# Three edits to one inference step of a hybrid trunk: activation rows of 388 columns, the last squares added ahead of the statistics, a packed product for the pool's shift

## The chip, the core and the metric

The kernel is one program on one core of a Trainium2 chip. The metric is the device time of one execution in microseconds. The names of engines are those of the profile: PE is TensorE (PEld its weight loads), DVE is VectorE, ACT is ScalarE, POOL is GpSimd, SP is SyncE, whose queue issues nearly all transfers (SPq). L521 is line 521 of the kernel before.

## What is computed

384 tokens (128 context tokens and 256 latent ones, each group with a conditioning vector of its own) go through four layers. Layers 0 and 3 mix tokens with a gated MLP in chunks (gMLP), layer 1 with centred pooling, layer 2 with windowed attention; each is followed by a feed-forward part with a width-3 convolution. Each sub-layer begins with an RMS norm and an adaLN scale and shift:

```python
def rms_norm(x, g):
    xf = x.astype(jnp.float32)
    y = xf * lax.rsqrt(jnp.mean(xf * xf, axis=-1, keepdims=True) + EPS)
    return (y * g.astype(jnp.float32)).astype(x.dtype)
...
        h = rms_norm(x, g_mix[i]) * (1 + sc1) + sh1
        if kind == 0:
            y = chunk_gmlp(h, a_w_in[j], a_g_v[j], a_w_s[j], a_b_s[j], a_w_out[j])
        elif kind == 1:
            y = multi_pool(h, p_w[j], p_b[j], p_scale[j])
...
        x = x + gt1 * y
        h = rms_norm(x, g_ffn[i]) * (1 + sc2) + sh2
        x = x + gt2 * conv_ffn(h, w_ffn_in[i], ffn_conv_w[i], ffn_conv_b[i], w_ffn_out[i])
```

The pooling mixer takes, for each of four groups of 256 features, the mean of h over a window of 2, 4, 8 or 16 tokens less h itself, and multiplies by a 256 x 256 matrix of the group.

## The kernel before

**Layout.** Features lie on partitions: x is 8 tiles (k or d, 0 to 7) of 128 features by 384 tokens. Weights stream in as chunks of 128 x 1024 float32 into five buffers (wraw, one SP transfer each). Each is split into two float32r parts: ScalarE rounds it (whi, L338), VectorE takes the remainder (wlo, L345). Activations are split in the same way into a high and a low part. A product is three passes, hi*hi, lo*hi and hi*lo (mm3, L631 to L638).

**hh and hl.** They hold a norm's operand for all eight feature tiles, 128 x 8 x TE with TE = 386: 384 tokens of x * g * (1 + sc), then two columns with the shift of each token group. A product with 386 moving columns so gives the shift's product beside the tokens', and the norm's factor (one per token) is applied after it. prep (L570) fills a tile d as soon as x_d is final: hh by ScalarE (L586), hl by VectorE (L588), then the square of x_d by ScalarE. VectorE adds the squares to acc (L468), but those of the last tile are only returned as sq. In layer 0's gMLP the products read the first 384 columns of the same rows.

**Statistics.** stats (L515) sums the squares over partitions by products with ones into cs: for each of three token tiles one product with acc and one with sq (L521). VectorE and ScalarE make 1/rms of it (L524, L508 to L512), VectorE a diagonal R of it (L530), and TensorE spreads R over all partitions (L536). This happens between the products of two feature tiles of the next phase: before tile 5, in layer 1's feed-forward part before tile 7 (stat_k), in layer 3's gMLP before tile 2.

**The pool** (L900 to L975). Its constants mx (mix) and the column sums ms (mixsum, two rows of 4 x 384) are loaded as it starts, into space that the feed-forward part before it has held. For a group g, first(g) makes the product with the group's weights, tokens on partitions; its fourth block is the shift's product, two rows (L929). scaled(g) copies the token blocks with the factor 1/rms (ScalarE, L938) and the two rows of the shift (VectorE, L940) to u. second(g) makes, for the group's two feature tiles, the product of u with the constants: a float32 product over two rows for the shift (L949), then three over tokens (L950, L953). VectorE adds the result to x (L956), and prep's work on that tile follows. The order is first(0), stats, first(1), scaled(0), first(2), scaled(1), second(0), scaled(2), first(3), second(1), scaled(3), second(2), second(3).

**What sets the order.** The program's text does: each engine runs its instructions in the order in which they are written, and waits on semaphores; SP's queue too. The pool's stretch of TensorE's chain begins at 540.38 us of the profile and ends where the feed-forward part's products begin, at 570.00.

Of the kernel before, what the change touches and what calls it, by code (L numbers as in the profile page):

```python
# [9 lines left out]
F32 = mybir.dt.float32  # L10
# [9 lines left out]
KD = 8  # L20
T = 384
# [13 lines left out]
TE = T + 2  # L35
BUFS = 5
# adaLN sections (layer, which of the six) computed along with the weights of a phase: by VectorE ("ad", features on
# partitions, dot products along the free axis) or by TensorE ("ap", column-tiled products)
# [18 lines left out]
# chunks of a phase that none of VectorE's sections follow, at its start and at its end  # L57
EDGES = {(0, "gv"): (2, 1), (0, "go"): (5, 0), (3, "gv"): (5, 2), "fi": (0, 6), (3, "go"): (5, 2)}

# the same for those of TensorE, at the end  # L60
# [4 lines left out]
# ---------------------------------------------------------------- packing  # L65


def out_chunks(fam, j, nk):
    """Two feature tiles at a time, but the last two one after the other."""
# [5 lines left out]
def weave(ws, es, lead, rest):  # L75
    """Spread es evenly over ws, but for the first `lead` and the last `rest`."""
# [13 lines left out]
def chunk_plan():  # L90
    """Chunks of 128 x 1024 in the order in which the program loads them: (family, index)."""
# [126 lines left out]
def shape_consts():  # L218
    """Constants that depend on shapes alone: rope tables, window mask, a selection matrix."""
# [20 lines left out]
def pool_mix():  # L240
    """mix[t', g, t]: weight of token t' in the centred mean at t, less one where t' = t."""
# [17 lines left out]
def pool_sums():  # L259
    """Column sums of mix for each group of tokens (what a shift common to all its tokens is weighed with)."""  # L260
# [7 lines left out]
# ---------------------------------------------------------------- program  # L268


class Prog:
# [36 lines left out]
    # ---- stream of chunks  # L308
# [4 lines left out]
    def load(self, most=BUFS):  # L313
        """Start the loads for which there is room."""
# [14 lines left out]
    def w_split(self, upto, mid=None):  # L329
        """Round the coming chunks (ScalarE), run mid, take the remainders (VectorE)."""  # L330
# [38 lines left out]
    # ---- adaLN parameters  # L369
# [37 lines left out]
    def ada_spare(self, n):  # L407
        """At most n of VectorE's chunks, of those already loaded."""
        for _ in range(n):
            if self.queue["ad"] and self.queue["ad"][0] in self.raw:  # L410
                self.ada_dve()
# [16 lines left out]
    def ada_fill(self, n, fin=True):  # L428
        """At most n products of those already loaded; without fin, none that would have to close a section before."""
# [17 lines left out]
    # ---- norm  # L447
    def residual(self, d, ps, l, ty, after):
        """x_d += gate * ps, and what follows from x_d."""
# [9 lines left out]
    def square(self, d, acc):  # L459
        """Add the squares of x_d to acc; the last ones are only returned."""  # L460
# [9 lines left out]

# [1111 lines left out]
```

## Time and profile before

| what | value |
|---|---|
| time, median of 3 runs | 1800.54 us (1800.51 to 1800.55) |
| profiled execution: span from first to last instruction | 1798.9 us |
| TensorE busy | 1778.0 us (99%), 10458 products |
| VectorE busy | 1364.0 us (76%) |
| ScalarE busy | 862.5 us (48%) |
| GpSimd busy | 1.8 us |
| mean DMA rate | 173 GB/s |

The span is that of one profiled execution; the runs' times are of other executions and include what lies before the first and after the last instruction. Busy times of products overlap, so the distance from one start to the next tells what a product costs, not its listed duration. A float32 product counts as two instructions (two passes), a float32r product as one.

### The profile page before, as it was taken

The page shows a single profiled execution, that of the slowest core. Times are in us where ns is not written, and L with a number is a line of the kernel's source. Part 1 is how long each engine was busy: PE and PEld are TensorE (multiplying, and loading weights), DVE is VectorE, ACT ScalarE, POOL GpSimd, SP SyncE. Part 2 cuts the span into 40 slices and gives each one's busy share as a digit, 9 for nine tenths or more (in the row PEclk, how much of TensorE's full clock was granted, in tenths as well). Part 3 has the DMA queues.
Part 4 walks back from the last instruction along what each step waited for, and adds up shares of the span by engine and source line. Part 5 has one row for each costly group of instructions (what it writes and reads, how often), then busy time and mean ns, then how long its engine had stood idle before and what let it go on. Part 6 is the DMA issues. An engine that isn't in the chain of part 4 may idle for free.

```text
span 1798.9 us, 27205 instructions
## 1 busy us (share of the span) xinstructions
PE 1778.0 (99%) x10458; PEld 1685.6 (94%) x10458; DVE 1364.0 (76%) x2568; ACT 862.5 (48%) x1470; POOL 1.8 (0%) x30
## 2 busy tenths in 40 slices
PE   7999999999999999999999999999999999999999
PEld 5799899999998999999678999999988999999999
DVE  5877688887776888776777788878776787888732
ACT  3634335554445555432568454544354443545431
POOL 0000000000000000000000000000000000000000
PEclk9999999999999999999999999999999999999999
DMA  8875565554553444365643444436546245444341
GB/s 321 281 243 178 211 219 182 184 177 157 205 182 118 152 153 164 135 211 184 241 171 124 145 154 154 162 135 211 193 161 213 96 163 188 141 145 148 123 148 58
DMA packets 87639, 311.67 MB, mean 173 GB/s; under 512 B 10451, under 2 KB 10963, under 8 KB 87253
## 3 DMA queue, kind: packets, MB, share of 16 engines
q1 hardware_dynamic: 87364, 309.92, 49.7%
q8 instruction: 82, 1.34, 0.3%
q14 instruction: 49, 0.39, 0.1%
q10 hardware_dynamic: 144, 0.01, 0.0%
HBM read 308.06 MB, written 1.84 MB: 172 GB/s over the span
## 4 chain that ended last, share of the span: by engine, by line
PE 96%; DVE 2%; ACT 1%; DMA 1%; issue 0%; DVEq 0%; ACTq 0%
PE mm L638 76%; PE mm L763 6%; PE S L1036 2%; PE S L638 1%; PE psa L398 1%; PE mm L807 1%; PE adaT L638 1%; PE mm L929 1%; PE psa L763 1%; PE adaT L763 1%; PE Tps L1036 1%; PE cs L521 1%; PE O L1256 0%; PE psa L638 0%; PE psa L1438 0%; PE Tps L1244 0%
## 5 line engine op out<-in xcount | busy, mean ns | idle before, releaser
L345 DVE TENSOR_TENSOR wlo<-wraw,whi 128x1024 fp32r<-128x1024 f32 (+2 forms) x390 | 466.0, 1201 | 212.2 <-ACT whi L338 207.1
L338 ACT ACTIVATE whi<-wraw 128x1024 fp32r<-128x1024 f32 (+2 forms) x390 | 400.7, 1036 | 388.4 <-PE mm L638 307.1
L638 PE MATMUL mm<-hh,whi 128*128 128x386 f32 (+1 forms) x1664 | 427.2, 342 | 0.0
L638 PE MATMUL mm<-hh,wlo 128*128 128x386 f32 (+1 forms) x1664 | 423.5, 339 | 0.0
L638 PE MATMUL mm<-hl,whi 128*128 128x386 f32 (+1 forms) x1664 | 421.2, 338 | 0.0
L638 PEld LDWEIGHTS mm<-hh,whi 128*128 128x128 f32 x1664 | 300.0, 188 | 7.9 <-issue 4.9
L638 PEld LDWEIGHTS mm<-hh,wlo 128*128 128x128 f32 x1664 | 303.4, 188 | 0.0
L638 PEld LDWEIGHTS mm<-hl,whi 128*128 128x128 f32 x1664 | 303.2, 188 | 0.0
L380 DVE SCALAR_TENSOR_TENSOR junk<-wraw,condb 128x1024 bf16<-128x1024 f32 x240 | 293.3, 1222 | 7.1 <-ACT condb L1500 2.7
L638 PE MATMUL mm<-gh,whi 128*128 128x384 f32 x704 | 193.6, 336 | 0.0
L638 PE MATMUL mm<-gh,wlo 128*128 128x384 f32 x704 | 193.6, 336 | 0.0
L638 PE MATMUL mm<-gl,whi 128*128 128x384 f32 x704 | 193.5, 336 | 0.0
L638 PEld LDWEIGHTS mm<-gh,wlo 128*128 128x128 f32 x704 | 128.5, 188 | 0.0
L638 PEld LDWEIGHTS mm<-gh,whi 128*128 128x128 f32 x704 | 128.5, 188 | 0.0
L638 PEld LDWEIGHTS mm<-gl,whi 128*128 128x128 f32 x704 | 128.4, 188 | 0.0
L682 ACT ACTIVATE ct<-ct 128x385 f32<-128x385 f32 x88 | 46.4, 528 | 156.7 <-DVE ct L676 156.6
L676 DVE SCALAR_TENSOR_TENSOR ct<-ab,par,ct 128x385 f32<-128x385 f32 x176 | 108.9, 621 | 12.2 <-ACT ct L674 8.2
L685 DVE SCALAR_TENSOR_TENSOR gg<-u,be,ct 128x128 f32<-128x128 f32 (+1 forms) x176 | 65.6, 416 | 47.6 <-ACT ct L682 47.6
L586 ACT ACTIVATE hh<-x,A 128x128 fp32r<-128x128 f32 x96 | 43.2, 457 | 102.5 <-DVE x L453 91.6
L672 ACT ACTIVATE ab<-a,be 128x128 f32<-128x128 f32 (+1 forms) x176 | 70.0, 446 | 28.9 <-DVE be L659 28.9
L657 DVE TENSOR_TENSOR a<-mm,rbs 128x384 f32<-128x384 f32 x88 | 48.7, 553 | 37.7 <-PE mm L638 31.8
L674 ACT ACTIVATE ct<-ab,par 128x385 f32<-128x385 f32 x88 | 62.7, 712 | 3.4
(302 smaller groups left out, 1987.6 us busy)
## 6 DMA issues: line engine op xcount, KB each, us to landing
wraw<-wts SPq DMA_DIRECT2D x562, 512.0 KB, 3.3
wraw<-wts SPq DMA_DIRECT2D x12, 256.0 KB, 2.5
wraw<-wts SPq DMA_DIRECT2D x8, 384.0 KB, 3.5
x<-x SPq DMA_DIRECT2D x4, 384.0 KB, 4.5
mx<-mix SPq DMA_DIRECT2D x1, 1280.0 KB, 8.1
y<-x SPq DMA_DIRECT2D x3, 384.0 KB, 3.1
condb<-condb SPq DMA_DIRECT2D x1, 1024.0 KB, 8.1
ws<-a_w_s SPq DMA_DIRECT2D x2, 512.0 KB, 4.2
```

Of the source, the lines that this page charges most:

```text
L338: nc.scalar.activation(hi[:, :n], t[:, :n], AF.Copy)
L345: nc.vector.tensor_tensor(out=lo[:, :n], in0=t[:, :n], in1=hi[:, :n].bitcast(F32), op=ALU.subtract)
L380: nc.vector.scalar_tensor_tensor(out=self.junk.bitcast(BF16), in0=w, scalar=1.0, in1=self.condb[:, c, :], op0=ALU.mult, op1=ALU.mult, accu ...
L638: nc.tensor.matmul(o, w[:, c:c + nw], r, start=(first and p == 0), stop=(last and p == 2))
L657: nc.vector.tensor_tensor(out=a1, in0=pa[:, 0:T], in1=rbs, op=ALU.mult)
L672: nc.scalar.activation(ab[:, p0:p1], a1[:, t0:t1], AF.Identity, bias=be[:, c:c + 1])
L674: nc.scalar.activation(t, ab[:, 1:T + 2], AF.Identity, scale=cw[1], bias=cb)
L676: nc.vector.scalar_tensor_tensor(out=t, in0=ab[:, i:i + T + 1], scalar=cw[i], in1=t, op0=ALU.mult, op1=ALU.add)
L682: nc.scalar.activation(t, t, GELU)
L685: nc.vector.scalar_tensor_tensor(out=g[:, t0:t1], in0=u1[:, t0:t1], scalar=be[:, 2 + c:3 + c], in1=t[:, t0 + c:t1 + c], op0=ALU.add, op1=A ...
L763: nc.tensor.matmul(ps[n][i], hs, w[p == 1][:, c:c + 512], start=(k == 0 and p == 0), stop=(k == 7 and p == 2))
L1036: nc.tensor.matmul(ps[i], hs, w[p == 1][:, c:c + 512], start=(k == 0 and p == 0), stop=(k == 7 and p == 2))
```

## The change

- hh and hl get rows of TP = 388 columns; the last two are never read. Products still have 386 columns (or 384 in layer 0).
- In each feed-forward part and in layer 3's gMLP, VectorE adds sq to acc (add_square) before the phase's first weights are asked for, and stats takes acc alone. The pool's and attention's statistics still take both.
- In the pool, the shift's product becomes one float32r product over 128 rows. msr holds the column sums rounded in rows 0, 1 and 32, 33 and the remainder in rows 64, 65; ush holds the shift's rows rounded in 0, 1 and 64, 65 and their remainder in 32, 33; all other rows are zero (filled by GpSimd). One pass so gives hi*hi, lo*hi and hi*lo.
- The small tiles dmy and ms have one buffer instead of two. Comments are gone.

```diff
+TP = T + 4
...
+    def add_square(self, pr):
+        self.nc.vector.tensor_tensor(out=pr["acc"], in0=pr["acc"], in1=pr["sq"], op=ALU.add)
...
-        d = self.tmp.tile([128, 1], F32, tag="dmy", name="dmy")
+        d = self.tmp.tile([128, 1], F32, tag="dmy", name="dmy", bufs=1)
...
-        m = self.tmp.tile([128, 3], F32, tag="ms", name="ms")
+        m = self.tmp.tile([128, 3], F32, tag="ms", name="ms", bufs=1)
...
             b = [self.bank()[:, :TE] for _ in range(4)]
+            self.add_square(pr)
             for kk in range(4):
                 w = self.w_get("fr")
...
-                        R = self.diag(self.stats(pr["acc"], pr["sq"]))
+                        R = self.diag(self.stats(pr["acc"]))
...
                 rbs = None
+                self.add_square(pr)
...
-                            R = self.diag(self.stats(pr["acc"], pr["sq"]))
+                            R = self.diag(self.stats(pr["acc"]))
...
-                        self.mm3([(b[i], 512 * k2 + 128 * i) for i in range(4)], w, (self.hh[:, k, :], self.hl[:, k, :]),
+                        self.mm3([(b[i], 512 * k2 + 128 * i) for i in range(4)], w,
+                                 (self.hh[:, k, 0:TE], self.hl[:, k, 0:TE]),
...
             nc.sync.dma_start(ms, self.a["mixsum"])
+            msr = pp.tile([128, 4, T], F32R, tag="msr", name="msr")
+            ush = pp.tile([128, 4, 256], F32R, tag="ush", name="ush")
+            nc.gpsimd.memset(msr.bitcast(F32), 0.0)
+            nc.gpsimd.memset(ush.bitcast(F32), 0.0)
+            for q in (0, 32):
+                nc.vector.tensor_copy(msr[q:q + 2], ms)
+            nc.vector.tensor_tensor(out=msr[64:66], in0=ms, in1=msr[0:2].bitcast(F32), op=ALU.subtract)
             res, aft = prep()
...
-                u = pp.tile([128, 4, 256], F32, tag="u", name="u", bufs=3)
+                u = pp.tile([128, 3, 256], F32, tag="u", name="u", bufs=3)
...
-                nc.vector.tensor_copy(u[0:2, 3, :], ps[1][0:2, 256:512])
+                for q in (0, 64):
+                    nc.vector.tensor_copy(ush[q:q + 2, g, :], ps[1][0:2, 256:512])
+                nc.vector.tensor_tensor(out=ush[32:34, g, :], in0=ps[1][0:2, 256:512], in1=ush[0:2, g, :].bitcast(F32),
+                                        op=ALU.subtract)
...
-                    nc.tensor.matmul(ps, u[0:2, 3, c], ms[:, g, :], start=True, stop=False, skip_group_check=True)
+                    nc.tensor.matmul(ps, ush[:, g, c], msr[:, g, :], start=True, stop=False, skip_group_check=True)
...
-        self.hh = self.const.tile([128, KD, TE], F32R, name="hh")
-        self.hl = self.const.tile([128, KD, TE], F32R, name="hl")
+        self.hh = self.const.tile([128, KD, TP], F32R, name="hh")
+        self.hl = self.const.tile([128, KD, TP], F32R, name="hl")
```

Where VectorE's instructions stand as the pool begins, before (x of the feed-forward part's last tile is just split into hh and hl; A are the gains, cs the statistics' sums, u the scaled copy):

```order
L588 SCALAR_TENSOR_TENSOR hl<-x,A,hh 128x256 [waits Activation_49]
L544 SCALAR_TENSOR_TENSOR A<-prm,par 128x16
L345 TENSOR_TENSOR wlo<-wraw,whi 128x1024 [waits DMAHW2_49,Activation_49]
L524 TENSOR_SCALAR ms<-cs 128x3 [waits PE_49]
L509 RECIPROCAL rs_5138<-rs_5137 128x3 [waits Activation_49]
...
L512 SCALAR_TENSOR_TENSOR rs_5140<-rs_5139,rs_5138 128x3 [waits DVE_49]
L940 COPY u<-mm 2x256 [waits Activation_49]
```

The same place in the changed kernel:

```order
L593 SCALAR_TENSOR_TENSOR hl<-x,A,hh 128x256 [waits Activation_49]
L926 CAST msr<-ms 2x1536 [waits DMAHW0_49,Pool_49]
L926 CAST msr<-ms 2x1536
L927 TENSOR_TENSOR msr<-ms,msr 2x1536 [waits DVE_49]
L549 SCALAR_TENSOR_TENSOR A<-prm,par 128x16
L346 TENSOR_TENSOR wlo<-wraw,whi 128x1024 [waits DMAHW2_49,Activation_49]
L529 TENSOR_SCALAR ms<-cs 128x3 [waits PE_49]
...
L517 SCALAR_TENSOR_TENSOR rs_5145<-rs_5144,rs_5143 128x3 [waits DVE_49]
L958 CAST ush<-mm 2x256 [waits Activation_49,Pool_49]
L958 CAST ush<-mm 2x256
L959 TENSOR_TENSOR ush<-mm,ush 2x256 [waits DVE_49]
```

Three operations over 1536 columns, the first of which waits for a transfer and for GpSimd, now stand ahead of the gains, a remainder and the statistics; one copy per group became two casts and a subtraction.

TensorE's statistics in layer 0's feed-forward part, before:

```order
L638 MATMUL mm<-hl,whi 128x386 x4
L521 MATMUL cs<-ones,acc 128x1 [waits PE_49]
L521 MATMUL cs<-ones,sq 128x1 [waits Activation_49]
L521 MATMUL cs<-ones,acc 128x1
L521 MATMUL cs<-ones,sq 128x1
L521 MATMUL cs<-ones,acc 128x1
L521 MATMUL cs<-ones,sq 128x1
L638 MATMUL mm<-hh,whi 128x386 x4
```

And in the changed kernel:

```order
L643 MATMUL mm<-hl,whi 128x386 x4
L526 MATMUL cs<-ones,acc 128x1 [waits DVE_49,PE_49]
L526 MATMUL cs<-ones,acc 128x1 x2
L643 MATMUL mm<-hh,whi 128x386 x4
L643 MATMUL mm<-hh,wlo 128x386 x4
```

Six products (twelve passes) became three, and they wait for VectorE's addition where they waited for ScalarE's square.

## Rows read from the trace of the kernel before

**Rows 1.** The page, part 4: the chain that ended last, by engine.

```profile
PE 96%; DVE 2%; ACT 1%; DMA 1%; issue 0%; DVEq 0%; ACTq 0%
```

**Rows 2.** Groups by form, TensorE: line, names, shapes, count | busy us, mean ns.

```profile
L638 PE MATMUL mm<-hh,whi 128*128 128x386 f32 x1536 | 393.1, 341 | 0.0
```

**Rows 3.** The chain in order of time: start us, us, what; gMLP and attention products.

```profile
164.21 8.44 PE mm L638 x48
...
995.34 16.66 PE S L638 x96
```

**Rows 4.** Timeline, TensorE, layer 2's feed-forward: start us, us; first product of each tile.

```profile
1047.58 0.52 PE L638 MATMUL mm<-hh,whi 128*128 128x386 f32 x2
...
1048.63 0.53 PE L638 MATMUL mm<-hh,whi 128*128 128x386 f32 x2
...
1049.70 0.51 PE L638 MATMUL mm<-hh,whi 128*128 128x386 f32 x2
...
1050.76 0.52 PE L638 MATMUL mm<-hh,whi 128*128 128x386 f32 x2
...
1051.83 0.52 PE L638 MATMUL mm<-hh,whi 128*128 128x386 f32 x2
...
1052.90 0.51 PE L638 MATMUL mm<-hh,whi 128*128 128x386 f32 x2
...
1053.96 0.51 PE L638 MATMUL mm<-hh,whi 128*128 128x386 f32 x2
...
1055.01 0.51 PE L638 MATMUL mm<-hh,whi 128*128 128x386 f32 x2
...
1056.07 0.52 PE L638 MATMUL mm<-hh,whi 128*128 128x386 f32 x2
```

**Rows 5.** The chain in order of time: statistics in layer 0's feed-forward part.

```profile
264.50 1.24 PE cs L521 x12
```

**Rows 6.** Timeline, TensorE, layer 1's feed-forward part: [idle before <-releaser].

```profile
589.33 0.88 PE L536 MATMUL adaT<-R,ones 128*128 128x384 f32 x2 [1.05 <-DVE R L530]
```

**Rows 7.** Groups by form, VectorE.

```profile
L468 DVE TENSOR_TENSOR acc<-acc,sq 128x384 f32<-128x384 f32 x42 | 23.5, 559 | 3.6 <-ACT sq L466 3.6
...
L800 DVE TENSOR_SCALAR v<-v,rd 128x512 f32<-128x512 f32 x16 | 6.6, 480 | 0.1
...
L940 DVE COPY u<-mm 2x256 f32<-2x256 f32 x4 | 1.6, 410 | 2.4 <-ACT u L938 2.4
```

**Rows 8.** Timeline, VectorE, start of layer 0's feed-forward part.

```profile
260.02 1.22 DVE L345 TENSOR_TENSOR wlo<-wraw,whi 128x1024 fp32r<-128x1024 f32 x1 [0.88 <-ACT whi L338]
```

**Rows 9.** The chain in order of time: first product of second(0), first of the feed-forward part.

```profile
550.21 0.84 PE mm L949 x2
...
570.00 12.72 PE mm L638 x72
```

**Rows 10.** Timeline, VectorE, the pool: a remainder; sums into two neighbouring feature tiles.

```profile
543.93 1.23 DVE L345 TENSOR_TENSOR wlo<-wraw,whi 128x1024 fp32r<-128x1024 f32 x1 [1.62 <-ACT whi L338]
...
564.79 0.72 DVE L956 SCALAR_TENSOR_TENSOR x<-mm,pgs,x 128x128 f32<-128x128 f32 x2
...
566.98 0.74 DVE L956 SCALAR_TENSOR_TENSOR x<-mm,pgs,x 128x128 f32<-128x128 f32 x2
```

**Rows 11.** Timeline, SP's queue: the issue of the pool's constants.

```profile
540.46 0.33 SPq L909 DMA_DIRECT2D mx<-mix  x1
```

**Rows 12.** The page, part 6: transfers, KB each, median us from issue to landing.

```profile
mx<-mix SPq DMA_DIRECT2D x1, 1280.0 KB, 8.1
```

**Rows 13.** Timeline, ScalarE, the pool: the first scaled copies.

```profile
546.38 1.20 ACT L938 ACTIVATE u<-mm,rs 128x256 f32<-128x256 f32 x3 [0.92 <-DVE rs L512]
```

**Rows 14.** The chain in order of time: the start of the kernel.

```profile
10.79 1.45 PE cs L521 x6
...
18.21 2.69 PE mm L763 x6
...
22.25 4.38 PE mm L763 x18
```

More of the change, by code (lines that the diff above doesn't have):

```diff
@@ L788, in vnorm @@
             def vnorm():
-                m = self.tmp.tile([128, 3], F32, tag="ms", name="ms")
+                m = self.tmp.tile([128, 3], F32, tag="ms", name="ms", bufs=1)
                 nc.vector.tensor_reduce(out=m, in_=ss, op=ALU.add, axis=AX.X)
@@ L1269, in store_lo @@
                                         op=ALU.subtract)
-            nc.scalar.activation(self.tmp.tile([128, 1], F32, tag="dmy", name="dmy"), self.ones[:, 0:1], AF.Exp)
+            nc.scalar.activation(self.tmp.tile([128, 1], F32, tag="dmy", name="dmy", bufs=1), self.ones[:, 0:1], AF.Exp)
             put(2)
@@ L1500, in hook @@
                 nc.scalar.activation(self.condb, self.condb, AF.Silu)
-                nc.scalar.activation(self.tmp.tile([128, 1], F32, tag="dmy", name="dmy"), self.ones[:, 0:1], GELU)
+                nc.scalar.activation(self.tmp.tile([128, 1], F32, tag="dmy", name="dmy", bufs=1), self.ones[:, 0:1], GELU)
         pr = None
```

## The prediction

> **What bounds the kernel.** The chain of work that ended last comes first: 96% of it is TensorE's [rows 1], so time is won or lost only where TensorE's products get fewer or shorter, or where it waits. The table of groups then says which products these are: 3 x 1536 = 4608 have 386 moving columns out of hh or hl [rows 2]. To see what one costs, I read starts, not the listed durations, since products overlap. 48 products of 384 columns out of hh (rows of 386) took 8.44 us, 175.8 ns each; 96 out of qS, whose rows are 384 long, took 16.66 us, 173.5 ns each [rows 3]. In the feed-forward stream, a block of 48 products of 386 columns runs from 1047.58 to 1056.07 us, 8.49 us or 176.9 ns each, and nothing is idle in it [rows 4].
>
> **Pitch 388.** No instruction is added. Two columns more than 384 should cost 173.5 x 386/384 = 174.4 ns; the block shows 176.9, so up to 2.5 ns of each product can be put down to where its row starts: 4608 x 2.5 = 11.5 us, all on the path. That is one end. The other is 0: if the number of columns does it, it stays. The block itself tells more. Each of its listed starts opens a feature tile k (six products). Counted from the start of hh, even k begin at multiples of 16 bytes already (3088 bytes per two rows), odd ones 8 bytes past one. Even tiles (the first listed and every second) took 1.05 + 1.06 + 1.07 + 1.05 = 4.23 us for 24 products, 176.25 ns; odd ones 1.07 + 1.07 + 1.06 + 1.06 = 4.26, 177.5 ns. If odd tiles only become like the even ones, each product gains half of 1.25, 0.63 ns, 2.9 us in all. But an even tile always follows an odd one, and a slow product can push the next, so I take the middle between 2.9 and 11.5: **-7.2 us**. No row excludes a loss by itself, but even tiles are not the slower ones, so I put the lower end at 0. Layer 0's 384 products of 384 columns show 175.8 against 173.5, 2.3 ns, 0.9 us at most; half of it, **-0.4**. ScalarE and VectorE write the same shapes at other offsets: nothing, and they are not on the path.
>
> The row above leaves even tiles 1.9 ns dearer than 174.4. The Trainium skill (SBUF — State Buffer, "SBUF: two separate sides", the note on cachelines) says that SBUF is read in lines of 16 bytes and that each access that crosses to a new line pays. By that rule a row of 386 float32, 96.5 lines, touches 97 whether it starts on a line or 8 bytes into one; pitch 388 would then give nothing for the 4608 products, and the sum would be that of the second rival below. The small difference of even and odd tiles speaks for it, layer 0's 384 columns neither way.
>
> **Squares added ahead.** Where both partial sums went into the statistics, six products run as twelve passes, 1.24 us of the chain [rows 5]; with one sum it is half, 0.62 us. It is done at five places: the four feed-forward parts and layer 3's gMLP. In layer 1's feed-forward TensorE waits 1.05 us right behind for VectorE's diagonal [rows 6]; there it would only wait longer, so that one is worth nothing. 4 x 0.62 = **-2.5 us**. The added VectorE addition has the shape of one of 559 ns [rows 7]; it stands where VectorE idles 0.88 us before its next remainder [rows 8], so I cost it at nothing. Without that cover, the first remainders of the next weights would come 0.6 us later, and they are chunks ahead of use. In layer 1 VectorE is late already and 0.6 us would show. The ms and dmy tiles with one buffer are rewritten long after their last reader: nothing.
>
> **Pool's packed product.** On TensorE, each of eight float32 products of two passes takes 0.84 us [rows 9]; one single-pass product of 384 columns takes 0.17 [rows 3]. 8 x 0.67 = 5.3 us less, if nothing else is late. Two things are.
> First, VectorE: a feature tile there costs 566.98 - 564.79 = 2.2 us [rows 10] against TensorE's 2.12, which falls to 1.45, so VectorE becomes the bound of the second half. The last two products need the last group's casts, which stand behind four tiles and two sets of three small copies (0.41 us each [rows 7]): 1.45 + 4 x 2.2 + 6 x 0.41 + 2 x 1.45 = 15.6 us from the first of these products to the feed-forward part, where 570.00 - 550.21 = 19.8 stand now [rows 9]. So 4.2 less; I take 4.0 for hand-overs.
> Second, the preparation of msr: two casts and a subtraction of 1536 columns stand on VectorE ahead of the gains, and wait for ms. The mixsum transfer is issued behind mix, at 540.46 [rows 11], on the same queue; mix takes 8.1 us to land [rows 12], so ms is there at about 548.6. A SBUF operation of 512 columns takes 480 ns [rows 7], a cast of 1536 by proportion 1.44; the subtraction is one and a half remainders of 1.23 us [rows 10], 1.85. VectorE is free at 548.6 + 4.7 = 553.3. Queued behind are the gains (a sixteen-column operation, 0.2), a remainder, the statistics' refinement and, on ScalarE, the three scaled copies: from 543.93 [rows 10] to 546.38 + 1.20 = 547.58 [rows 13], 3.65 us. The first packed product can start at 557.1 instead of 550.2: TensorE idles 6.9 us. If the casts go at twice that rate, it is 5.5; if they go at the subtraction's, 7.8; if ms landed at its issue, there is no stall, and the pool gains its 4.0. GpSimd's two fills have no row of that size; they start with the transfers, and I take them as done within its 8 us. Together 6.9 - 4.0 = **+2.9 us**.
>
> **Sum.** -7.2 - 0.4 - 2.5 + 2.9 = -7.2 us. The span of the profiled execution is 1798.9 us; the median of the runs is 1800.54, and 1.6 us lie outside the span. Put on the median: **1793.3 us**, with an own range of 1790 to 1797.5 (the ends of the casts and half of the pitch's uncertainty). About 0.2%, 3.6 us, is what a measurement of this kernel can tell from no change.
>
> **Rivals.**
> *The whole excess goes.* All rows of 388 then read like rows of 384: -11.5 - 0.9 - 2.5 + 2.9 = -12.0, 1788.5. For it: rows of 384 run at a constant 173.5. Against it: even tiles, already at 16 bytes, are not much better.
> *The pitch does nothing.* The columns' number, not the start, costs the 2.5 ns: -2.5 + 2.9 = +0.4, 1800.9. For it: even and odd tiles differ by 0.7% only. Against: layer 0's products have 384 columns and still cost 2.3 ns more than qS's. The SBUF page's rule on lines, above, leads here.
> *Slower: the stall lowers the clock.* TensorE's longest wait inside the stream is 1.05 us [rows 6], and the stream goes on at its pace. At the start, after a long idle time, six products of 512 columns took 2.69 us, 0.45 each, while 18 of them later took 4.38, 0.24 each [rows 14]: the lower of the two levels, 1.2 against 2.4 GHz, held from TensorE's first work at 10.79 to about 20.9 us. If a stall of 7 us has the same effect in the pool, the products behind it run at half speed for 4 us (18.21 to 22.25) up to 10 us, and lose 2 to 5 us; part is covered by VectorE, I take 3. With casts at the slow rate (+0.9) and no gain from the pitch: -2.5 + 2.9 + 0.9 + 3.0 = +4.3, 1804.8. It decides only if the pitch gives under 1 us. The Trainium skill (TensorE: Matmul & The Clock Gate, "HAM oscillation") states that an idle TensorE falls back to the lower clock; no stretch of this trace has an idle time that long after the start, so it is untested here.
> *The stall doesn't come.* If mixsum lands ahead of mix, the pool gains 4.0 instead of losing 2.9: -14.1, 1786.4. Against it: one queue, issue order.
>
> **Chances.** Forecast 0.34, whole excess 0.18, pitch nothing 0.28, slower 0.14, no stall 0.06. Faster: 0.06 + 0.18 + 0.30 of the forecast's 0.34 = 0.54. Within 0.2%: the other 0.04 and 0.26 of the second rival = 0.30. Slower: 0.14 and the 0.02 left of that rival = 0.16. A range from 1786 (the case without a stall) to 1804 leaves out the slower case and the tails.
>
> **What would show it.** Right: the block of 48 products near 8.42 us (176.9 - 1.6 ns each) instead of 8.49; the statistics' group halved at five places; layer 1's wait for the diagonal grown to 1.6 us; a wait of TensorE of 5.5 to 7.8 us before the first packed product, ended by VectorE, whose casts of msr end their wait on a DMA at about the same distance from the mix issue; the feed-forward part of layer 1 some 3 us later after the pool's start. Wrong: the block still at 8.49, or at 8.37 (174.4 each) throughout; no TensorE wait in the pool; spacings of 0.3 us and more behind it.

## The result and the profile after

The changed kernel takes 1810.41 us (median of 4 runs, 1809.58 to 1810.81) where the kernel before takes 1800.53: a ratio of 1.0051, 95% interval 1.0039 to 1.0063 (the ratios here and below are not quotients of the two medians, and differ from them by up to 0.0006). By the medians it is slower by 9.9 us. The forecast was 1793.3 us with a range of 1786 to 1804: wrong in sign, and outside the range.

TensorE still sets the end, as in [rows 1] (the page's part 4, chain by engine, after):

```profile
PE 95%; DVE 2%; DMA 2%; ACT 1%; issue 0%; SPq 0%; DVEq 0%; ACTq 0%
```

To find the stage that lost the time I compare, in the two traces, when the statistics' products (cs) start; they stand once in each sub-layer. gh and gl are the high and low parts of a feed-forward part's hidden features, the operands of its output product, whose stream follows that out of hh and hl. The stretch from the pool's statistics to those of the feed-forward part behind it holds the pool. Distances in us, from the profiled execution of each:

| stretch between statistics | before | after | difference |
|---|---|---|---|
| feed-forward 0 (its products out of gh and gl included) | 278.69 | 279.70 | +1.01 |
| pool, to feed-forward 1 | 41.63 | 48.09 | +6.46 |
| feed-forward 1 | 268.30 | 269.90 | +1.60 |
| attention | 177.79 | 177.91 | +0.12 |
| feed-forward 2 | 273.91 | 274.92 | +1.01 |
| gMLP of layer 3 | 220.78 | 220.03 | -0.75 |
| feed-forward 3, to the end | 273.50 | 274.45 | +0.95 |

Two things stand out. The pool lost 6.5 us where I had +2.9. And every feed-forward part lost 1 to 1.6 us where I had a gain from the pitch. Groups by form say which products did: those out of hh barely changed (341 ns, [rows 2]), but those out of gh and gl, which the change doesn't touch, have grown. Before (line, names, shapes, count, busy us, mean ns):

```profile
L638 PE MATMUL mm<-gh,whi 128*128 128x384 f32 x704 | 193.6, 336 | 0.0
```

After:

```profile
L643 PE MATMUL mm<-hh,whi 128*128 128x386 f32 x1536 | 392.6, 341 | 0.0
...
L643 PE MATMUL mm<-gh,whi 128*128 128x384 f32 x704 | 196.0, 340 | 0.0
```

Starts tell what they cost. TensorE's timeline at the first products out of gh, layer 0, before:

```profile
448.70 0.51 PE L638 MATMUL mm<-gh,whi 128*128 128x384 f32 x2
449.04 0.51 PE L638 MATMUL mm<-gh,wlo 128*128 128x384 f32 x2
449.39 0.51 PE L638 MATMUL mm<-gl,whi 128*128 128x384 f32 x2
449.74 0.51 PE L638 MATMUL mm<-gh,whi 128*128 128x384 f32 x2
```

and after:

```profile
446.99 0.52 PE L643 MATMUL mm<-gh,whi 128*128 128x384 f32 x2
447.35 0.52 PE L643 MATMUL mm<-gh,wlo 128*128 128x384 f32 x2
447.70 0.52 PE L643 MATMUL mm<-gl,whi 128*128 128x384 f32 x2
448.05 0.52 PE L643 MATMUL mm<-gh,whi 128*128 128x384 f32 x2
```

Two products take 0.347 us before and 0.353 after. In the full list of starts the products out of gh and gl stand 173, 173, 174 ns apart before (mean 173.33 over the 528 of a part) and 174, 179, 174, 179 after (mean 176.67), from the first to the last, in all four parts. 2112 x 3.34 = 7.05 us. Nothing waits in either.

The pool, by the chain in order of time (start us, us, what):

```profile
540.51 0.33 SPq L917
540.88 6.39 DMA ms<-mixsum
547.37 0.95 DVE msr L926
...
549.31 1.75 DVE msr L927
551.07 0.18 DVE A L549
551.25 1.13 DVE wlo L346
...
561.60 2.92 PE mm L946 x24
564.52 0.17 PE mm L969
564.70 0.22 PE mm L970 x2
564.92 0.88 PE mm L973 x4
...
571.73 0.42 DVE ush L959
572.29 0.66 PE mm L969
572.95 0.43 PE mm L970 x2
573.38 1.71 PE mm L973 x4
...
576.52 12.73 PE mm L643 x72
```

The forecast's wait is there: the transfer of the column sums, the casts, the subtraction, the remainder and the statistics stand one behind the other. TensorE's timeline has two waits in the pool, and behind them the one for layer 1's diagonal:

```profile
556.35 0.66 PE L969 MATMUL mm<-msr,ush 128*128 128x384 f32 x1 [6.09 <-DVE ush L959]
...
572.29 0.66 PE L969 MATMUL mm<-msr,ush 128*128 128x384 f32 x1 [2.73 <-DVE ush L959]
...
595.86 0.89 PE L541 MATMUL adaT<-R,ones 128*128 128x384 f32 x2 [1.69 <-DVE R L535]
```

And the clock fell in each of the two waits and stayed low behind it. Each row is a stretch, its length and the busy time (with the number of instructions) of PE, PEld, DVE, ACT and POOL; then come the granted clock (1.00 is 2.4 GHz, 0.50 is 1.2), the DMA engines' busy share and GB/s:

```profile
545.00:554.80 9.80, 5.27 (x45) 4.59 (x44) 5.69 (x10) 1.40 (x5) 0.00 (x0) 1.00 0.33 119
554.90:561.70 6.80, 5.35 (x16) 4.66 (x17) 5.26 (x12) 3.25 (x7) 0.00 (x0) 0.50 0.21 80
561.70:571.90 10.20, 7.86 (x52) 6.89 (x51) 8.27 (x21) 6.12 (x15) 0.00 (x0) 1.00 0.00 1
572.00:575.30 3.30, 3.01 (x9) 2.66 (x10) 3.01 (x10) 1.85 (x5) 0.00 (x0) 0.50 0.00 0
```

The same four products (L973) take 0.88 us at one level and 1.71 at the other, in the chain above.

The statistics became what was forecast. Timeline, layer 0's feed-forward part, against the 1.24 us of [rows 5]:

```profile
263.42 0.72 PE L526 MATMUL cs<-ones,acc 128*128 128x1 f32 x6
264.00 0.96 PE L643 MATMUL mm<-hh,whi 128*128 128x386 f32 x4
```

From the first to what follows: 0.58 us.

### The profile page after: what moved, and what is told of

It is laid out like the page before. It is cut to its first block, busy times and chain, and to the rows that moved or that the text cites. A ratio compares the mean times of both kernels' runs of the same rounds, so it can differ in the third digit from the quotient of the medians.

```text
span 1808.4 us, 27156 instructions
## 1 busy us (share of the span) xinstructions
PE 1778.0 (98%) x10420; PEld 1690.9 (94%) x10420; DVE 1373.2 (76%) x2584; ACT 862.7 (48%) x1470; POOL 4.0 (0%) x32
## 4 chain that ended last, share of the span: by engine, by line
PE 95%; DVE 2%; DMA 2%; ACT 1%; issue 0%; SPq 0%; DVEq 0%; ACTq 0%
PE mm L643 76%; PE mm L769 6%; PE S L1056 2%; PE S L643 1%; PE psa L399 1%; PE mm L813 1%; DMA wraw<-wts 1%; PE adaT L643 1%; PE psa L769 1%; PE adaT L769 1%; PE Tps L1056 1%; PE O L1276 0%; PE psa L643 0%; PE Tps L1264 0%; PE psa L1458 0%; PE mm L973 0%
## 6 DMA issues: line engine op xcount, KB each, us to landing
mx<-mix SPq DMA_DIRECT2D x1, 1280.0 KB, 10.1
```

## The experiments

Theories for gh and gl: **inherited phase** (two patterns are possible for the same products, and a stream keeps the one into which the stream before it ended) against **placement** (their addresses, which moved with hh's size, make them slow). Times are medians, with the kernel before's median from the same chip; ratios carry 95% intervals. "Pool" is the distance between statistics of the table above.

**1. rows386.** The changed kernel, pitch undone.

```diff
-TP = T + 4
+TP = T + 2
```

> The changed kernel, but hh and hl with rows of 386 columns again (squares, packed pool product and one-buffer tiles stay). Theory 'inherited phase' (the feed-forward output products, gh and gl, 384 columns at a constant pitch, can run at 173.3 ns each or at an alternating 174 and 179 ns, 176.7 on average, and keep the pattern with which the stream of hh products before them ended): the stream before them is the kernel before's again, so 173.3 ns and about -7 us, while hh's products go back from 176.8 to 176.95 ns (+0.7 us): 1804 us in all. Rival 'placement' (gh and gl got slower because all tiles behind hh moved against each other): gh still stands 64 bytes nearer to the weights than before, because the small tiles keep one buffer, so it stays at 176.7 ns and the time at 1811 us. If the distance doesn't matter but the absolute place does, 1804 us too.

Measured: 1803.59 us beside 1801.74, ratio 1.0011 (1.0002 to 1.0020). gh and gl at 173.33 ns in all four parts, hh at 176.9. Placement by distance falls; the pool costs 48.8 us here too.

**2. break_before_out.** The changed kernel; memory stays as it is.

```diff
         self.ada_need(l, ty)
+        if fam == "fo":
+            brk = self.px.tile([128, 3], F32, tag="px", name="brk")
+            self.nc.tensor.matmul(brk[:, 0:1], self.ident, self.ones[:, 0:1], start=True, stop=True)
```

> The changed kernel with one small product (128 x 1, result not used) ahead of the first product out of gh in each of the four feed-forward parts; nothing moves in memory. 'Inherited phase': the small product breaks the stream, the products out of gh and gl start anew and run at 173.3 ns instead of 176.7: 2112 x 3.34 ns = -7.05 us, plus 4 x about 0.15 us for the product: 1804.0 us. 'Placement': the pattern belongs to the addresses, so 176.7 ns and 1811.0 us.

Measured: 1803.17 us beside 1801.74, 1.0006 (0.9996 to 1.0015): some 7 us of the change's loss gone for four small products. gh and gl at 173.5 ns on average with the first interval, 173.3 behind it. Placement is out.

**3. pitch_alone.** The kernel before with rows of 388 columns (and dmy and ms with one buffer).

```diff
+TP = T + 4
...
-        self.hh = self.const.tile([128, KD, TE], F32R, name="hh")
+        self.hh = self.const.tile([128, KD, TP], F32R, name="hh")
```

> The kernel before with rows of 388 columns and the two small tiles with one buffer (which make room for them), nothing else. The prediction on record: -7.2 - 0.4 = 1792.9 us. After the result, both theories: hh's products 176.8 ns instead of 176.95 (-0.7 us), layer 0's a little less (-0.2 us); gh's and gl's products 176.7 instead of 173.3 (+7.05 us) if the pitch alone decides how the stream before them ends: 1806.7 us. If gh and gl stay at 173.3 ns here, it was the statistics or the pool that set their pattern: 1799.6 us.

Measured: 1807.57 us beside 1801.74, 1.0030 (1.0018 to 1.0041). hh at 176.80 ns, gh and gl at 176.67 in all four parts. The pitch alone brings the slow pattern; alone it is a loss of some 5.8 us.

**4. squares_alone.** The kernel before with add_square and stats of acc alone, at the five places of the change's diff.

> The kernel before with the last squares added by VectorE ahead of the statistics, nothing else. The prediction's term: four places of 0.62 us, -2.5 us: 1798.0 us, with the statistics' chain entries halved at five places and layer 1's wait for the diagonal grown to about 1.6 us. By 'inherited phase' the shorter statistics stand some 36 feature rows ahead of gh, so the pattern of the hh stream has settled again by then: gh at 173.3 ns, 1798.0 us; if it had not settled, gh goes to 176.7 ns in some layers, +1.76 us for each.

Measured: 1798.87 us beside 1801.74, 0.9982 (0.9973 to 0.9991). By stretches -0.67, -0.67, -0.70 and -0.68 us in feed-forward 0 and 2, layer 3's gMLP and feed-forward 3, and -0.02 in layer 1's: -2.7 us. gh and gl stay at 173.33 ns. In this trace attention, which the edit leaves as it is, took 180.5 us instead of 177.8: TensorE waited 1.74 us for ScalarE's hh, and the clock stood at 0.50 for 3.4 us behind. rows400_squares (below) shows the same, 180.2 us and a wait of 1.59. So whole traces differ by some 3 us for reasons outside an edit, and the stretches are the better measure.

**5. break_inside.** Where in the stream does a break have to be? The same small product, but between the first two pairs of feature tiles.

```diff
+            if fam == "fo" and m == 1:
+                brk = self.px.tile([128, 3], F32, tag="px", name="brk")
+                self.nc.tensor.matmul(brk[:, 0:1], self.ident, self.ones[:, 0:1], start=True, stop=True)
             b = banks(m)
```

> The changed kernel with the one small product not ahead of gh's stream but inside it, between the first two pairs of feature tiles (after 132 of 528 products). 'Inherited phase', in its strict form (a pattern holds until anything breaks it): the first 132 products at 176.7 ns, the other 396 at 173.3: 4 x 396 x 3.34 ns = -5.3 us, some 1805 us. Rival 'start only' (what counts is that gh's first products start from a pause): 176.7 ns before and after the small product, 1811 us.

Measured: 1806.45 us in one run beside 1801.13. All four parts: 132 products at 174 and 179 ns, then 396 at 173.3. TensorE's timeline at the break (the spacings in ns are from the list of starts; rounded to hundredths of a microsecond they show only in the durations, 0.52 ahead of it and 0.51 behind):

```profile
469.44 0.52 PE L643 MATMUL mm<-gh,wlo 128*128 128x384 f32 x2
469.79 0.52 PE L643 MATMUL mm<-gl,whi 128*128 128x384 f32 x2
470.14 0.28 PE L737 MATMUL brk<-ones,ident 128*128 128x1 f32 x2
470.28 0.60 PE L643 MATMUL mm<-gh,whi 128*128 128x384 f32 x2
470.72 0.51 PE L643 MATMUL mm<-gh,wlo 128*128 128x384 f32 x2
471.07 0.51 PE L643 MATMUL mm<-gl,whi 128*128 128x384 f32 x2
```

The trace of the changed kernel has the same thing by itself, in attention's output product: until 1003.26 us the products out of qS stand 174 and 179 ns apart, two small adaLN products come between, and from 1003.83 on they stand 173 to 174 apart.

```profile
1002.55 0.52 PE L643 MATMUL S<-qS,wlo 128*128 128x384 f32 x2
1002.90 0.52 PE L643 MATMUL S<-qS,whi 128*128 128x384 f32 x2
1003.26 0.38 PE L422 MATMUL adaT<-ident,adarow 128*128 128x128 f32 x2
1003.39 0.60 PE L643 MATMUL S<-qS,whi 128*128 128x384 f32 x2
1003.83 0.51 PE L643 MATMUL S<-qS,wlo 128*128 128x384 f32 x2
1004.17 0.86 PE L643 MATMUL S<-qS,whi 128*128 128x384 f32 x4
```

**6 and 7. rows400 and rows392.** What is a row's start worth to hh's own products? The changed kernel with other pitches (rows392 has T + 8); the diagonal R shares another small tile's buffers to make room.

```diff
-TP = T + 4
+TP = T + 16
...
-        R = self.tmp.tile([128, 3, 128], F32, tag="R", name="R", bufs=1)
+        R = self.tmp.tile([128, 3, 128], F32, tag="ct", name="R")
```

> The changed kernel with rows of 400 columns (1600 bytes, so that every row of hh and hl starts at the same place modulo 64 bytes, as gh's rows do); the diagonal R shares the buffers of another small tile to make room. Theory 'row start' (which the prediction's pitch term rests on): with equal starts the 386-column products reach 173.3 x 386 / 384 = 174.2 ns instead of 176.8: 4608 x 2.6 = -12.0 us, layer 0's 384-column products 173.3 instead of 175.4, -0.7 us. Rival 'columns': two more than 384 cost it, whatever the start: hh stays at 176.8 ns, and only layer 0's products gain. In either case gh and gl start from another end of the hh stream: 176.7 ns (1810.4 us in all by 'columns', 1797.7 by 'row start') or 173.3 ns (1803.4 and 1790.7).

> The changed kernel with rows of 392 columns (1568 bytes: starts at two places modulo 64 bytes; R shares a buffer as in rows400). Rows of 386, 388 and 400 columns gave hh's 386-column products 176.94, 176.80 and 175.85 ns. Theory 'ladder' (the fewer different places modulo 64 bytes the rows start at, the fewer products are late): between the last two, 176.0 to 176.7 ns. Rival 'only equal places help' : 176.8 as with 388. gh and gl again at 173.3 or at 176.7 ns, by how the stream before them ends; nothing says which.

Measured: rows400 1799.74 us beside 1800.77, 0.9989 (0.9980 to 0.9999); hh 175.85 ns, gh and gl 173.33, layer 0's products of 384 columns 174.2 (175.7 before). rows392 1809.56 beside 1801.30, 1.0047 (1.0031 to 1.0063); hh 176.81, gh and gl 176.67. Neither theory is right: 400 columns give 0.95 ns of the 2.6 hoped for, and 392 nothing over 388, so the ladder falls.

**8. pool_alone.** The kernel before with the packed product, its preparations as in the change, and one buffer for dmy and ms; the diff shows the product alone.

```diff
-                nc.tensor.matmul(ps, u[0:2, 3, c], ms[:, g, :], start=True, stop=False, skip_group_check=True)
+                nc.tensor.matmul(ps, ush[:, g, c], msr[:, g, :], start=True, stop=False, skip_group_check=True)
```

> The kernel before with the pool's packed product and the one-buffer tiles alone (rows of 386, squares as before). The prediction's term was +2.9 us. By the trace of the changed kernel it is +6.5 us (from the statistics of the pool to those of the feed-forward part behind it 48.1 us instead of 41.6): 1807.0 us, with a TensorE wait of about 6 us before the first packed product, one of about 2.7 us before the last group's, and two stretches at the lower clock. Rival: part of the +6.5 us comes with the pitch or with the squares (the wait for the diagonal in layer 1), then 1804 to 1806 us.

Measured: 1806.25 us beside 1800.77, 1.0032 (1.0020 to 1.0045). Pool 47.48 us, +5.85, waits of 6.09 and 3.16 us, two stretches at clock 0.50. So the loss is the packed product's own. It isn't the same in each run: with the pool's code as in the change the distance is 45.5 (rows392) to 48.9 us (break_before_out), by when the column sums land and by how long the clock stays at 0.50 (below).

**9. waits_filled.** The changed kernel with TensorE busy in its waits (the products' results are not used).

```diff
+            def fill(n):
+                ps = self.ps_bank()
+                for _ in range(n):
+                    nc.tensor.matmul(ps[:, :T], w[0][:, 0:128], hh[:, 7, 0:T], start=True, stop=True)
...
+            fill(34)
             second(0)
...
+            fill(14)
             second(3)
```

> The changed kernel with TensorE kept at work in its two waits of the pool: 34 products of 384 columns (results not used) ahead of second(0) and 14 ahead of second(3). The data come as late as before, only TensorE isn't idle. Theory 'clock': the lower clock after each wait costs time of its own; 5.3 us and 3.1 us of products then run at 2.4 GHz instead of 1.2: up to 2.7 + 1.5 = 4.2 us less, 1806.2 us, and no stretch at the lower clock in the pool. Rival 'VectorE is the bound there anyway': VectorE's casts, additions and remainders stand in a row from 554.9 to 574.4 us, so the clock costs little: 1809.5 to 1810.5 us.

Measured: 1810.96 us beside 1800.77, 1.0051 (1.0036 to 1.0066). The clock stays at 1.00:

```profile
554.90:561.70 6.80, 5.88 (x40) 5.31 (x39) 5.86 (x14) 4.15 (x10) 0.00 (x0) 1.00 0.29 104
```

From the first packed product to the feed-forward part it is 17.67 us, where the changed kernel's trace has 19.82. The other runs with this pool fall in line with the time that TensorE's work in that part ran at clock 0.50:

| runs | work at clock 0.50, us | first packed product to feed-forward part, us |
|---|---|---|
| waits_filled | 0 | 17.7 |
| rows392, rows400, pool_alone | 3.6, 4.4, 5.0 | 18.1, 18.6, 18.6 |
| sums_first, after | 8.1, 8.4 | 19.8, 19.8 |
| break_before_out, rows386, break_inside | 9.3, 9.5, 9.6 | 20.4, 20.3, 20.4 |

So the clock costs 0.5 to 2.7 us, 2.15 against the changed kernel's trace: half of what the first theory allowed, and more than the rival did. In the profiled execution, the fastest of four (1808.43 us), the pool is 46.8 us, 1.3 less than in the changed kernel's trace: against the 2.15 stand the casts of the column sums, which began 0.94 us later after the statistics (5.18 against 4.24 us). The other three executions took 1810.9 to 1812.5 us and were not profiled: why the median gained nothing stays open.

**10. sums_first.** As experiment 2, and the small transfer goes first.

```diff
-            nc.sync.dma_start(mx, self.a["mix"])
             nc.sync.dma_start(ms, self.a["mixsum"])
+            nc.sync.dma_start(mx, self.a["mix"])
```

> The changed kernel with the small product ahead of gh (as in break_before_out) and the transfer of the column sums issued ahead of mix instead of behind it. By the prediction's working VectorE waits for that transfer: 24 KB issued first should land some 2 us after 540.5, the casts and the subtraction run 542.5 to 546.2, and the first packed product starts at about 552 instead of 556.4: -4 us against break_before_out, and less time at the lower clock on top (up to -2.7): 1796.5 to 1799.2 us where break_before_out gives 1803.2. Rival: the transfer waits for something other than the queue (the room that the feed-forward part frees, or mix's bytes all the same): 1803 us.

Measured: 1800.96 us beside 1800.77, 0.9996 (0.9986 to 1.0005). Pool 45.8 us, against 48.9 in experiment 2. The first packed product starts 10.4 us after the statistics, where it is 12.4 to 14.2 in the runs with the other order. The place in the queue was part of the reason for the late transfer: it takes 3.88 us from its issue, where the changed kernel's trace has 6.39, so the first wait goes from 5.68 us (experiment 2) to 3.20, not to nothing, and the clock falls all the same. The transfer has 12 KB, not the 24 that I wrote. The gain of 4 us or more that I expected over experiment 2 did not come: the pool's stretch gained 3.1, the medians, each less its own kernel before, 1.2. TensorE's two waits:

```profile
552.49 0.41 PE L972 MATMUL mm<-msr,ush 128*128 128x384 f32 x1 [3.20 <-DVE ush L962]
567.59 0.66 PE L972 MATMUL mm<-msr,ush 128*128 128x384 f32 x1 [2.82 <-DVE ush L962]
```

**11. pool_tuned.** The kernel before with the squares and a packed product whose preparations are moved: the column sums' transfer goes first, their casts stand behind the statistics, and ScalarE makes the two casts of each group's shift. Against the changed kernel's pool:

```diff
-            nc.sync.dma_start(mx, self.a["mix"])
             nc.sync.dma_start(ms, self.a["mixsum"])
+            nc.sync.dma_start(mx, self.a["mix"])
...
-            for q in (0, 32):
-                nc.vector.tensor_copy(msr[q:q + 2], ms)
-            nc.vector.tensor_tensor(out=msr[64:66], in0=ms, in1=msr[0:2].bitcast(F32), op=ALU.subtract)
...
-                    nc.vector.tensor_copy(ush[q:q + 2, g, :], ps[1][0:2, 256:512])
+                    nc.scalar.activation(ush[q:q + 2, g, :], ps[1][0:2, 256:512], AF.Copy)
...
             r = self.stats(pr["acc"], pr["sq"])
+            for q in (0, 32):
+                nc.vector.tensor_copy(msr[q:q + 2], ms)
+            nc.vector.tensor_tensor(out=msr[64:66], in0=ms, in1=msr[0:2].bitcast(F32), op=ALU.subtract)
```

> The kernel before with the squares added ahead and the packed product in the pool, but the column sums' transfer goes first, their casts stand behind the statistics on VectorE's queue instead of ahead, and ScalarE makes the two casts of each group's shift. By the theory that the packed product lost its 5.3 us on TensorE to VectorE's queue (casts ahead of the statistics, then two small operations more per group) and to the late transfer, TensorE waits under 1 us before the first packed product and the pool takes 1 to 4 us less than in the kernel before (from statistics to statistics 38 to 40.6 us; 41.6 before, 48.1 in the changed kernel): 1794 to 1797 us. Rival: VectorE's eight feature tiles at 2.2 us bind the second half whatever stands ahead: 41 to 42 us, 1797.5 to 1798.5 us.

Measured: 1796.67 us beside 1801.30, 0.9974 (0.9963 to 0.9985). Pool 39.9 us, 1.7 less than before and 8.2 less than in the changed kernel. The first wait is down to 0.19 us; the one before the last group is still there:

```profile
548.78 0.44 PE L963 MATMUL mm<-msr,ush 128*128 128x384 f32 x1 [0.19 <-DVE ush L953]
562.27 0.41 PE L963 MATMUL mm<-msr,ush 128*128 128x384 f32 x1 [2.83 <-DVE ush L953]
```

**12 to 14. What paid, together.** rows400_squares and rows416_squares are the kernel before with the squares and rows of 400 or 416 columns (to make room R shares buffers as in rows400, and the second keeps one buffer for the norms' small tiles); all_together is the second with the pool of experiment 11.

> The kernel before with rows of 400 columns and the squares added ahead, but its own pool: what paid in the other runs, without what cost. hh's products 175.85 instead of 176.94 ns, 4608 x 1.09 = -5.0 us; layer 0's 384-column products -0.5 us; squares -2.5 us; gh and gl at 173.3 ns as in rows400: -8.0 us, 1792.5 us where the kernel before takes 1800.5. If gh and gl fall into the alternating pattern, +7.05: 1799.6 us.

> As rows400_squares, but with rows of 416 columns (1664 bytes: starts at one place modulo 128 bytes, at four modulo 512); the small tiles of the norms keep one buffer to make room. 'Ladder' carried on: hh's products below 175.85 ns, 174.2 at best, which would be up to 4608 x 1.65 = -7.6 us against rows400_squares: 1785 to 1792 us. Rival: 64 bytes are all that matters, 175.85 ns, 1792.5 us. With gh and gl in the alternating pattern +7.05 us in either case.

> rows416_squares with the pool of pool_tuned: rows of 416 columns, squares added ahead, packed product with its preparations moved. If the parts add up: -10.6 us (1801.3 to 1792.2 less the pool's 1.7 us) against the kernel before, ratio 0.9938 to 0.994. Rival: another end of the pool's stretch or of a stream puts gh and gl into the alternating pattern: +1.76 us for each feed-forward part that does.

| run | us, beside before | ratio (interval) | hh, ns | gh and gl, ns |
|---|---|---|---|---|
| rows400_squares | 1794.56, 1801.30 | 0.9958 (0.9941 to 0.9974) | 175.85 | 173.4 |
| rows416_squares | 1792.17, 1801.30 | 0.9947 (0.9932 to 0.9962) | 175.56 | 173.3 |
| all_together | 1790.07, 1801.13 | 0.9937 (0.9921 to 0.9954) | 175.56 | 173.3 |

The parts add up: all_together is 11 us faster than the kernel before and 20 faster than the change. Rows of 416 give 0.29 ns over 400, not the 1.65 that I allowed at best. A block of 48 products out of hh in layer 2's feed-forward part, rows416_squares, first and last start (8.43 us, where [rows 4] have 8.49):

```profile
1044.80 0.51 PE L642 MATMUL mm<-hh,whi 128*128 128x386 f32 x2
...
1053.23 0.51 PE L642 MATMUL mm<-hh,whi 128*128 128x386 f32 x2
```

The lists of starts tell more, feature tile by feature tile (k). Means in ns per product, over the 60 passes through the eight tiles in the three long streams of 386-column products (feed-forward 1 to 3, 959 products in each list):

| row pitch (run) | k = 0 | 1 | 2 | 3 | 4 | 5 | 6 | 7 |
|---|---|---|---|---|---|---|---|---|
| 386 (before) | 175.1 | 179.2 | 176.2 | 177.8 | 179.0 | 177.1 | 174.3 | 176.8 |
| 388 (changed kernel) | 177.6 | 176.8 | 177.4 | 175.0 | 175.4 | 176.7 | 177.5 | 178.0 |
| 400 (rows400) | 176.5 | 176.9 | 175.8 | 174.2 | 176.5 | 177.0 | 175.7 | 174.2 |
| 416 (rows416_squares) | 176.1 | 175.0 | 176.1 | 175.0 | 176.1 | 175.0 | 176.1 | 175.0 |

Rows of 400 columns start at four places modulo 256 bytes and their means repeat after four tiles; rows of 416 start at two, and their means repeat after two. With 386 and 388 columns no two of the eight starts agree, and nothing repeats. The weights are laid out alike in all four.

## Why the prediction was wrong, step by step

**Pitch (-7.2 us): the step that failed.** In the three long streams the products out of hh and hl went from 176.95 to 176.80 ns, 4608 x 0.15 = -0.7 us; the block of [rows 4] has 8.48 us after against 8.49. Timeline, first and last start of that block in the changed kernel:

```profile
1055.17 0.52 PE L643 MATMUL mm<-hh,whi 128*128 128x386 f32 x2
...
1063.65 0.52 PE L643 MATMUL mm<-hh,whi 128*128 128x386 f32 x2
```

Two inferences were weak. One read the 1.25 ns between even and odd tiles as the price of a start 8 bytes off. By the table the even tiles of the kernel before range from 174.3 to 179.0 ns, so their mean says little; with all rows on 16 bytes the tiles still differ, and the even ones are now the dearer (177.0 against 176.6). The other put the whole distance to 174.4 ns down to starts and took a multiple of 16 bytes for a good one. Starts do go with the price, at a coarser step: tiles that start alike modulo 256 bytes agree within 0.05 ns, others differ by up to 2.8 (rows400), and the cheapest, at 174.2, cost no more than their columns. 388 columns moved the dear places to other tiles and left the mean. No run puts all rows at one place modulo 256 bytes, so how much of the distance can go stays open, and so does the reason.

The rival "the pitch does nothing" had the result for 388 columns right. The Trainium skill's rule on lines (SBUF — State Buffer, "SBUF: two separate sides": lines of 16 bytes; by it a row of 386 columns touches 97 of them either way) agrees with 386, 388 and 392 columns (176.95, 176.80 and 176.81 ns). The same rule says nothing of the 1.1 and 1.4 ns that 400 and 416 columns bring, where 97 lines are touched as well; there the measurement decides. Nor are layer 0's 384 columns neutral by it, as I wrote: they touch 96 lines from a line's start and 97 from 8 bytes into one, but no gain shows (see Layer 0 below).

**What the sum left out: +7.05 us.** I said that a slow product can push the next, but only within hh's stream. The sum priced each stream by itself, so products whose operands, shapes and waits don't change got no term. The runs show that they take 173.3 or 176.7 ns with the same operands at the same addresses, that the pitch of the stream before them decides which, and that they hold it for hundreds of products until something comes between. That the end of the stream before hands over a state is the reading that fits all of this; what the state is was not seen. It is the largest term of the difference; without it the change would still have been some 2.9 us slower.

**Layer 0 (-0.4).** 175.7 to 175.5 ns, 384 products: -0.1 us. Even that isn't shown to be the pitch's: rows of 386 with the change's other small tiles take 175.3 (rows386, pool_alone).

**Squares (-2.5).** Right in size and places: -2.7 by stretches in squares_alone, nothing in layer 1, where TensorE's wait for the diagonal grew from the 1.05 us of [rows 6] to 1.69 (forecast 1.6). The added sums cost VectorE nothing that shows.

**Pool (+2.9): half right.** The stall came, by the named chain, at nearly the named length: 6.09 us, forecast 6.9, range 5.5 to 7.8. That it came so near is in part luck. The casts took 0.95 us each, not 1.44, the subtraction 1.75 (1.85 forecast), and the column sums were there at 547.3, not 548.6, so VectorE was free at 551.07, 2.2 us before the forecast's 553.3. But from there to the first packed product it took 5.3 us, not 3.8: the casts and the subtraction of the first group's shift (554.90 to 556.20) were not in the sum. Nor did the sums wait until all of mix had landed, as I had assumed: in this trace mix, issued at 540.51, landed at 550.6, behind them (the changed kernel's page, part 6: KB, us from issue to landing):

```profile
mx<-mix SPq DMA_DIRECT2D x1, 1280.0 KB, 10.1
```

The saving behind the stall (-4.0) failed. From the first packed product to the feed-forward part I had 15.6 us against 19.8 [rows 9]. Those 19.8 are the chain's starts; by the timeline's it was 19.5 before and 19.8 after, a loss of 0.3. So of the pool's +6.46 us, 6.1 lie ahead of the first packed product and 0.3 behind it. 2.15 us of the distance to the forecast are the clock (waits_filled; 0.5 to 2.7 in the other runs). The other 2 are, by the order of the trace, work that my list of VectorE's steps left out: the remainder of the next chunk (1.2 us) stands between the first two groups' casts, and VectorE waits for ScalarE's copies ahead of a group's casts (0.53 us, twice); no run takes these out one by one. With casts moved off its queue the stretch is 16.9 us (pool_tuned).

**The slower rival** was the one that came: "the stall lowers the clock", with its condition that the pitch gives under 1 us. Its clock term (3 us) was near the 2.15 measured. Its pool, 6.8 us in all, was near the 6.46 measured partly by luck: the casts were not slow (its 0.9 us), and the saving that it kept did not come. It reached 1804.8 and had a chance of 0.14; with the 7 us of gh and gl it is about what happened. The Trainium skill (TensorE: Matmul & The Clock Gate, "HAM oscillation") says that an idle TensorE falls back to the lower clock; the trace agrees: 0.50 in the rows at the waits of 6.09 and 2.73 us. The rival "the stall doesn't come" failed: the column sums did land ahead of mix, which was its condition, but only 3.3 us ahead, too late to spare the stall. sums_first shows the issue order to be the cause of somewhat under half of the wait.

The terms add up to -0.7 - 0.1 - 2.7 + 7.05 + 6.46 = +10.0 us, where the medians differ by 9.9. In the two traces the stretches of the table make +10.4 us and the part ahead of them, the start and layer 0's gMLP, -0.9, of which only the 0.1 is explained. That part ends anywhere from 262.8 to 264.3 us in the 16 traces, so the sum is good to about 1 us.

## What to carry to other kernels

Where one stream of products follows another without a gap, list the starts of both streams, not only of the one that is edited: the untouched one can change its spacing by 2% for its whole length, and one tiny product between them is a cheap test. Before giving TensorE a cheaper product, write down the queue of the engine that must prepare it, transfer included, and place the preparation behind what TensorE waits for next. A gain argued from alignment wants a second and third pitch, and the mean of each row by itself, before it is believed.

## What the runs showed of the hardware that was not expected

- Equal products (384 columns, same operands, same addresses) have two steady spacings: 173.3 ns, or 174 and 179 in turn. Each held for as long as the stream ran (up to 528 products); one product of 128 x 1, or two small ones of another part, ended the slow one at once. With nothing in between, it was always the slow one after hh streams with rows of 388 and 392 columns, and always the fast one after 386, 400 and 416. Why a pitch leads to one or the other was not settled.
- Products of 386 columns never became steady: mostly 169 to 186 ns from one to the next, with means from 175.56 to 176.95 ns by pitch. A tile's mean, 174.2 to 179.2 ns, repeated where rows start alike modulo 256 bytes (rows of 400 and 416 columns).
- The granted clock fell to 0.50 at every wait of TensorE of 3.2 to 6.3 us in the pool, and at most of those of 2.7 to 2.9 us; in rows392 and rows400 a wait of 2.8 us left it at 1.00. In attention it fell behind waits of 1.74 and 1.59 us (squares_alone, rows400_squares), and not behind one of 1.78 (rows400). So the length of a wait alone did not decide it. With the data as late but TensorE at work in the pool's waits it stayed at 1.00.
- A transfer of 12 KB was issued right behind one of 1280 KB on the same queue, and the cast that waited for it began 5.6 to 7.4 us after its issue. The large one took 6.4 to 10.1 us, so the small one landed before it in most traces. Issued ahead of the large one, it took 3.9 us.
